# Silu from ScalarE's table, a two-row substitution and block copies in the token mixers of a hybrid decoder layer

## The chip, the core and the metric

The kernel runs on one core of a Trainium2 chip. The core has five engines that run their own instruction lists and wait for each other by semaphores: TensorE (PE in the profile; its weight loads are PEld), VectorE (DVE), ScalarE (ACT), GpSimd (POOL) and SyncE (SP), which here issues the DMAs. The metric is the device time of one execution in microseconds, as the median of several runs. All data are float32; the large matrix products are run as three products of split operands in the type fp32r.

## The reference

One decoder layer (DEPTH is 1) over 2048 tokens of width 1024. Cut to what the change touches:

```python
qkv = jax.nn.silu(causal_depthwise_conv(qkv, gdn_conv[i]))
q_a, k_a, v_a = jnp.split(qkv, 3, axis=-1)          # 4 heads of 128; q_a, k_a are L2-normed
g_dec = -jnp.exp(gdn_a_log[i]) * jax.nn.softplus(a_gdn + gdn_dt_bias[i])
o_a = gated_delta_rule_chunked(q_a, k_a, v_a, g_dec, beta)
o_a = o_a * lax.rsqrt(mean(o_a * o_a) + EPS) * gdn_norm[i] * jax.nn.silu(z_gdn)
...
f = lb + (1 - lb) * sigmoid(f_pre)                  # log_f of the reference
k_b = (1.0 - lb) * jax.nn.sigmoid(-f_pre)
o_b = hgrn2_chunked(jax.nn.silu(q_hg), k_b, i_hg, log_f)
o_b = o_b * lax.rsqrt(mean(o_b * o_b) + EPS) * hgrn_norm[i] * jax.nn.silu(g_hg)
```

The gated delta rule needs, for every chunk of tokens, the solution of a unit lower triangular system. The mixers are followed by an output projection, a squared-ReLU MLP and a gated embedding; the change leaves these alone.

## The kernel before

The work goes in four quarters `q` of 512 tokens (`QT`), each of four chunks (`NC`) of 128. Activations lie transposed: features on the partitions, tokens along the free axis.

The trace falls into stages. Up to about 45 us the embedding products and the first operands are made. From there to about 1180 us runs the input projection with the mixers inside it. Then come the output projection (to about 1440 us), and the two MLP products and the gate product (to the end). The change lies in the mixers and in the constants that they read.

**Projection and mixers.** The list `works` holds 33 products for each quarter: one for the decays, and for each of four heads eight (`KINDS`: k, q, v, z of the delta rule; f, i, q, g of HGRN2). One work is 24 matmuls on L927, in `SPT` = 3 parts, and after each part `tick()` advances a clock and runs one step of every generator that is due. The due times stand in the tuples `A_STEPS`, `I_STEPS` and `B_STEPS` (`A_LAST`, `B_LAST` for the last head): the generator `gdn_mixer` of a head is advanced at these distances from the head's start, `hgrn_mixer` likewise. A head's eight works take 24 steps and its delta-rule mixer ends at step 59, so the mixers of two or three heads are open at once.

The order of PE's instructions is that of the program (`manual_schedule`), and so is SP's inside the loop: what a step issues to PE stands there between the matmuls of the projection, and when it has to wait, everything behind it waits. The order on DVE, ACT and POOL is made by a planner ahead of time, from when it reckons that operands are ready; on the chip each engine takes its list in order.

**The activations.** There is no silu function in use: `silu2` (L475) computes Tanh of half the argument on ACT and then `(th + 1) * x` on DVE (L479), which is twice the silu. `conv_silu` (L490) uses it for k, q and v, `to_hq` (L789) for HGRN2's queries. `gate` (L509) does the same for z and g with a Copy on ACT that carries half the norm's gain (L514) and a product on DVE (L515). The factor of two is made up for by `4 * EPS` and the like in the norms.

**The delta-rule head (`gdn_mixer`).** The decays come by DMA into `gf`. The matrix `e` of decay ratios is made by four DVE instructions (L552, one a chunk) and one Exp (L553). `u`, the strictly triangular system, is formed on DVE (L591) from matmuls of k with itself. Its diagonal blocks of 32 (`SB`) go through DRAM into the tile `sys`, so that 16 blocks lie on 128 partitions; rows are then solved one after the other, each by a product (L615) and a sum (L616) on DVE, 31 pairs for a head. The result goes through DRAM into `xx`, which holds for each chunk the inverse (right half) and its transpose (left half, made by DVE's transposes on L630). Two levels, 32 and 64, join the blocks: `um` gets the off-diagonal blocks of `u` (ACT, L634), PE forms `psp` (L638), ACT copies it to `pt` (L640), PE multiplies again into `psd` (L647, L648, L655), and DVE adds `psd` to `xx` (L651, L656). The matmuls stream all 128 columns. Then the four chunks follow in sequence: `psa`, `r` on DVE (L664), `psb` with the inverse, `w` on ACT (L669), the state `S` on DVE (L674).

**The HGRN2 head (`hgrn_mixer`).** Levels 1 to 64 (`LEVELS`) build the attention of a chunk. On each level PE multiplies k with the odd blocks of q (L726), DVE scales the odd blocks of q (L727) and the even blocks of k (L729), and a predicated copy with the level's mask puts the result into `att` (L732). The masks are stored for all four chunks, 256 columns each. `to_f` (L767) makes f and k from a Tanh by two DVE instructions (L773, L774).

**The end of a head (`finish`, L518).** The squared output is summed by PE, its inverse root is spread through DRAM, and DVE multiplies the gated output by it (L530).

## Time and profile before

| | us |
|---|---|
| median of 3 runs | 2867.37 (2864.68 to 2872.71) |
| the profiled execution, device time | 2865.62 |
| its span | 2863.8 |
| PE busy / DVE busy / ACT busy in the span | 2773.0 / 2158.2 / 1331.2 |
| PE busy in L927, the input projection | 791.2 |
| DVE busy in L615 and L616, the substitution | 136.1 and 111.0 |

Rows of the profile read as follows. A group has the line, the engine, the operation, output and inputs by their names (with the head's part of the name cut, so `psp_g` stands for all heads), the shapes and the count; then the busy time in us, the mean of one in ns, and the idle time of the engine just before it with the engine or DMA that ended it. A row of the list of waits has who waited, for whom, the total in us, how often, and the longest. A row of the timeline has start and length in us and, in brackets, the idle time before it. A float32 matmul shows as two instructions. Matmuls overlap, so the distance from start to start tells more than the length. The granted clock is TensorE's, 1.00 at full speed.

### The profile page before, as it was taken

To read this page: it belongs to the slowest core of one execution; us is meant where nothing else is said; L and a number is where in the kernel's file an instruction comes from. 1 tells how busy PE (TensorE), PEld (TensorE's weight loads), DVE (VectorE), ACT (ScalarE), POOL (GpSimd) and SP (SyncE) were. 2 spreads that over 40 slices of the span, in tenths; PEclk is the share of its full clock that TensorE was granted. 3 is DMA by queue.
4 is the path that set the end of the run, shared out by engine and by line. 5 is a ranking of instruction groups with operands and counts; after the bars stand their busy time and mean duration, and the time that the engine had idled before them with its cause. 6 is when DMAs were issued, how large, how long until landed. Compare 5 with 4: busy or idle time off the path is not lost.

```text
span 2863.8 us, 39544 instructions
## 1 busy us (share of the span) xinstructions
PE 2773.0 (97%) x13361; PEld 2293.7 (80%) x13361; DVE 2158.2 (75%) x4712; ACT 1331.2 (46%) x2460; POOL 108.7 (4%) x104
## 2 busy tenths in 40 slices
PE   7899999999999999999989999999999999999999
PEld 5688788888888888777768887888888888887887
DVE  6688787887878887758887886776787765567675
ACT  6354334333333333457555655554555445465431
POOL 0000000000000000000000000000100000001000
PEclk9999999999999999999999999999999999999999
DMA  7666667655665666587755646666564446577573
GB/s 254 223 222 205 215 213 246 201 199 201 224 195 190 212 199 196 159 284 247 258 173 192 229 166 209 217 212 210 193 210 139 148 157 213 188 255 239 196 230 116
DMA packets 268602, 589.70 MB, mean 206 GB/s; under 512 B 55642, under 2 KB 59960, under 8 KB 249072
## 3 DMA queue, kind: packets, MB, share of 16 engines
q1 hardware_dynamic: 268400, 587.18, 61.5%
q8 instruction: 106, 1.74, 0.3%
q14 instruction: 96, 0.79, 0.1%
HBM read 420.14 MB, written 166.92 MB: 205 GB/s over the span
## 4 chain that ended last, share of the span: by engine, by line
PE 46%; DVE 3%; DMA 3%; issue 2%; ACT 2%; POOL 0%; SPq 0%; DVEq 0%; ACTq 0%; POOLq 0%
PE u L996 21%; PE d L996 18%; PE mmg L996 6%; DMA da<-sumd 1%; DMA raw_out<-in_w_out_dram 1%; DMA xo<-in_xT_dram 1%; DMA b<-h1d 0%; PE mmo L996 0%; DVE w_out L162 0%; DVE t L162 0%; ACT L1033 0%; ACT L1032 0%; ACT w_out L161 0%; DVE b L1143 0%; POOL acc_y L225 0%
## 5 line engine op out<-in xcount | busy, mean ns | idle before, releaser
L927 PE MATMUL mm<-xt,w 128*128 128x512 f32 x3072 | 791.2, 405 | 2.6 <-ACT w L161 1.2
L927 PEld LDWEIGHTS mm<-xt,w 128*128 128x128 f32 x3072 | 564.6, 191 | 122.8 <-ACT w L161 1.6
L996 PE MATMUL d<-db,da 128*128 128x512 f32 x2688 | 613.0, 390 | 4.2 <-DVE db L215 3.2
L996 PE MATMUL u<-t,wu 128*128 128x512 f32 x2604 | 603.4, 393 | 3.3 <-ACT wu L161 3.2
L996 PEld LDWEIGHTS d<-db,da 128*128 128x128 f32 x2688 | 504.0, 188 | 112.6 <-DVE db L215 5.8
L996 PEld LDWEIGHTS u<-t,wu 128*128 128x128 f32 x2604 | 488.8, 188 | 117.2 <-ACT wu L161 4.1
L215 DVE TENSOR_TENSOR db<-db 128x512 fp32r<-128x512 f32 x224 | 160.8, 718 | 69.9 <-ACT db L214 69.4
L1325 DVE TENSOR_TENSOR u<-u,u 128x512 f32<-128x512 f32 x224 | 150.8, 684 | 72.1 <-PE u L996 71.0
L996 PE MATMUL mmo<-mixT,w_out 128*128 128x512 f32 x720 | 171.5, 398 | 9.1 <-DVE w_out L162 6.8
L214 ACT ACTIVATE db<-db 128x512 fp32r<-128x512 f32 x224 | 140.9, 629 | 78.7 <-DMA db<-hid 76.3
L996 PE MATMUL mmg<-h2T,wg 128*128 128x512 f32 x768 | 177.5, 393 | 0.0
L996 PEld LDWEIGHTS mmo<-mixT,w_out 128*128 128x128 f32 x720 | 137.0, 191 | 42.6 <-DVE w_out L162 8.5
L996 PEld LDWEIGHTS mmg<-h2T,wg 128*128 128x128 f32 x768 | 144.2, 188 | 32.8
L1366 ACT ACTIVATE u<-u 128x512 f32<-128x512 f32 x128 | 80.9, 632 | 179.6 <-DVE u L1325 179.2
L162 DVE TENSOR_TENSOR da<-da 128x512 fp32r<-128x512 f32 x128 | 94.3, 737 | 91.0 <-ACT da L161 90.5
L615 DVE TENSOR_TENSOR pr_g<-xs_g,sys_g 128x4 f32<-128x4 f32 (+30 forms) x496 | 136.1, 274 | 29.3 <-DMA sys_g<-ud_g 19.3
L161 ACT ACTIVATE da<-da 128x512 fp32r<-128x512 f32 x128 | 80.5, 629 | 140.0 <-DMA da<-sumd 117.3
L616 DVE TENSOR_REDUCE xs_g<-pr_g 128x4 f32<-128x8 f32 (+30 forms) x496 | 111.0, 224 | 9.8
L161 ACT ACTIVATE wu<-a 128x512 fp32r<-128x512 f32 x124 | 73.9, 622 | 46.7 <-DMA a<-in_w_up_dram 44.6
L225 POOL TENSOR_TENSOR acc_y<-acc_y,sq_y 128x512 f32<-128x512 f32 x28 | 38.7, 1382 | 1389.4 <-ACT sq_y L224 1389.4
L162 DVE TENSOR_TENSOR wu<-a,wu 128x512 fp32r<-128x512 f32 x124 | 84.9, 688 | 4.0 <-ACT wu L161 4.0
L726 PE MATMUL at_h<-q_h,k_h 128*128 128x64 f32 x640 | 82.6, 273 | 3.2 <-DVE tail_g L548 1.7
(364 smaller groups left out, 3893.1 us busy)
## 6 DMA issues: line engine op xcount, KB each, us to landing
w<-cache_in SPq DMA_DIRECT2D x96, 1024.0 KB
db<-hid SPq DMA_DIRECT2D x224, 256.0 KB
cache_in<-w SPq DMA_DIRECT2D x32, 1024.0 KB
hid<-u SPq DMA_DIRECT2D x128, 256.0 KB
da<-sumd SPq DMA_DIRECT2D x128, 256.0 KB
a<-in_w_up_dram SPq DMA_DIRECT2D x124, 256.0 KB
hid<-ht SPq DMA_DIRECT2D x96, 256.0 KB
dr<-in_w_down_dram SPq DMA_DIRECT2D x96, 256.0 KB
```

The costliest lines, as they stand in the source:

```text
L161: S.activation(t[:, 0], raw, AF.Copy)
L162: eng.tensor_tensor(t[:, 1], raw, t[:, 0], ALU.subtract)
L214: S.activation(t[:, 0], plain(t), AF.Copy)
L215: V.tensor_tensor(t[:, 1], plain(t), t[:, 0], ALU.subtract)
L225: eng.tensor_tensor(acc, acc, sq, ALU.add)
L615: V.tensor_tensor(pr[:, :, 0:i], xs[:, :, 0:i], sys[:, None, 0:i, i].broadcast_to([P, GC, i]), ALU.mult)
L616: V.tensor_reduce(xs[:, :, i], pr[:, :, 0 : i + 1], AX.X, ALU.add)
L726: PE.matmul(ps[:, c, :], k[:, blk(c)], odd, start=True, stop=True)
L927: PE.matmul(ps, *terms[i], start=i == 0, stop=i == nt - 1)
L996: PE.matmul(ps, a, b, start=start, stop=stop)
L1325: V.tensor_tensor(c[new], c[old], ps, ALU.add)
L1366: S.activation(c[k], c[k], AF.Relu)
```

## The change

- `silu2` goes. k, q, v and HGRN2's q take the function Silu on ACT; `gate` becomes one Silu, and the norm's gain is multiplied in at `finish`. The factors of 2 and 4 go from the norms.
- `e` is made by one DVE addition over all chunks and four Exp with the negative decay as bias.
- The substitution solves two rows a step: one product and one sum for rows i and i+1, and a third small instruction that adds row i's share to row i+1.
- In the inverse, `psp` and `psd` are formed for the wanted half of the columns only, `part` is a strided view of the tile `half`, and ACT copies the new blocks into `xx` where DVE added whole tiles.
- HGRN2's q and k lie in one tile `qk`, and one DVE instruction scales both. f and k come from ACT (Identity).
- The masks are stored once and broadcast over the chunks.

```diff
-N_CONST = C_MASK + 2 * len(LEVELS)
+N_CONST = C_MASK + (len(LEVELS) + 1) // 2
...
+            V.tensor_scalar(gcol[:, :, 4:8], gcol[:, :, 0:4], -1.0, None, ALU.mult)
...
-            silu2(y, acc, name)
+            S.activation(y, acc, AF.Silu)
...
-            S.activation(th, ps, AF.Tanh, scale=0.5)
-            S.activation(zt, ps, AF.Copy, scale=gate_w[:, n : n + 1])
-            V.scalar_tensor_tensor(zt, th, 1.0, zt, ALU.add, ALU.mult)
+            S.activation(zt, ps, AF.Silu)
...
-            V.tensor_tensor(og, og, rsb, ALU.mult)
+            V.scalar_tensor_tensor(og, og, col(R_GNORM if h < 4 else R_HNORM), rsb, ALU.mult, ALU.mult)
...
+            V.tensor_tensor(e, gf, over_chunks(negm), ALU.add)
             for c in range(NC):
-                V.scalar_tensor_tensor(e[:, c, :], gf[:, c, :], gc[:, c : c + 1], negm, ALU.subtract, ALU.add)
-            S.activation(e, e, AF.Exp)
+                S.activation(e[:, c, :], e[:, c, :], AF.Exp, bias=gcol[:, c, 4 + h : 5 + h])
             S.activation(gf, gf, AF.Exp)
...
-            for i in range(1, SB):
-                V.tensor_tensor(pr[:, :, 0:i], xs[:, :, 0:i], sys[:, None, 0:i, i].broadcast_to([P, GC, i]), ALU.mult)
-                V.tensor_reduce(xs[:, :, i], pr[:, :, 0 : i + 1], AX.X, ALU.add)
-                if i % 4 == 3:
+            for i in range(0, SB, 2):
+                if i:
+                    V.tensor_tensor(pr[:, :, :, 0:i], xs[:, None, :, 0:i].broadcast_to([P, 2, GC, i]),
+                                    sys[:, 0:i, i : i + 2].rearrange("p j two -> p two j")[:, :, None, :]
+                                    .broadcast_to([P, 2, GC, i]), ALU.mult)
+                    V.tensor_reduce(xs[:, :, i : i + 2].rearrange("p g two -> p two g"), pr[:, :, :, 0 : i + 1],
+                                    AX.X, ALU.add)
+                V.scalar_tensor_tensor(xs[:, :, i + 1], xs[:, :, i], sys[:, i, i + 1 : i + 2], xs[:, :, i + 1],
+                                       ALU.mult, ALU.add)
+                if i % 4 == 2:
                     yield
...
+                psp = bank(f"psp_{n}_{lev}", pp)[:, : QT // 2].rearrange("p (c b s) -> p c b s", c=NC, s=s)
+                left = xx[:, :, :P].rearrange("p c (b two s) -> p c b two s", two=2, s=s)[:, :, :, 0]
+                right = xx[:, :, P:].rearrange("p c (b two s) -> p c b two s", two=2, s=s)[:, :, :, 1]
+                part = half.rearrange("p c (b two s) -> p c b two s", two=2, s=s)[:, :, :, 0]
                 for c in range(NC):
-                    PE.matmul(psp[:, blk(c)], um[lev][:, c, :], xx[:, c, :P], start=True, stop=True)
-                pt = m2.tile([P, NC, P], F32, tag="pt", name=f"pt_{n}_{lev}", bufs=1)
-                S.activation(flat(pt), psp, AF.Copy)
+                    PE.matmul(psp[:, c], um[lev][:, c, :], left[:, c], start=True, stop=True)
+                S.activation(part, psp, AF.Copy)
                 yield
...
+                psd = bank(f"psd_{n}_{lev}", pp).rearrange("p (c two b s) -> p c two b s", c=NC, two=2, s=s)
+                for c in range(NC):
+                    if lev == 5:
+                        PE.matmul(psd[:, c, 0], xx[:, c, P:], part[:, c], start=True, stop=True)
+                    PE.matmul(psd[:, c, 1], half[:, c, :], right[:, c], start=True, stop=True)
+                for i in range(P // (2 * s)):
+                    o = 2 * s * i
+                    if lev == 5:
+                        S.activation(left[o + s : o + 2 * s, :, i], psd[o + s : o + 2 * s, :, 0, i], AF.Copy)
+                    S.activation(right[o : o + s, :, i], psd[o : o + s, :, 1, i], AF.Copy)
...
-                V.tensor_tensor(qv[:, :, 1, :], qv[:, :, 1, :],
-                                gv[:, :, 0:1].broadcast_to([P, nb, s]), ALU.mult)
-                V.tensor_tensor(kv[:, :, 0, :], kv[:, :, 0, :],
-                                gv[:, :, 1:2].broadcast_to([P, nb, s]), ALU.mult)
+                sides = bass.AP(qk.tensor, qk.offset + s, [qk.ap[0], [QT - s, 2], [2 * s, nb], [1, s]])
+                V.tensor_tensor(sides, sides, gv.rearrange("p n two -> p two n")[:, :, :, None]
+                                .broadcast_to([P, 2, nb, s]), ALU.mult)
...
-            V.tensor_scalar(f, th, ha[:, h : h + 1], hb[:, h : h + 1], ALU.mult, ALU.add)
-            V.tensor_scalar(k, th, hna[:, h : h + 1], ha[:, h : h + 1], ALU.mult, ALU.add)
+            S.activation(f, th, AF.Identity, scale=ha[:, h : h + 1], bias=hb[:, h : h + 1])
+            S.activation(qk[:, 1], th, AF.Identity, scale=hna[:, h : h + 1], bias=ha[:, h : h + 1])
...
-            silu2(qq, ps, f"qh{q}_{h}")
-            b["q"] = qq
+            S.activation(b["qk"][:, 0], ps, AF.Silu)
```

## The prediction, made before the result was known

> **What bounds the kernel now.** I read three views in this order: the page's busy shares, the busy times of the mixer stage alone, and the list of what TensorE waited for there. First the page, then the stage from 45 to 1215 us (columns: stretch, length, then busy us and count for PE, PEld, DVE, ACT, POOL, then granted clock, DMA share, GB/s):

> ```profile
> PE 2773.0 (97%) x13361; PEld 2293.7 (80%) x13361; DVE 2158.2 (75%) x4712; ACT 1331.2 (46%) x2460; POOL 108.7 (4%) x104
> ```

> ```profile
> 45.00:1215.00 1170.00, 1125.79 (x6234) 956.71 (x6232) 937.58 (x2817) 446.89 (x1008) 64.17 (x67) 0.98 0.62 206
> ```

> The whole diff lies in this stage. PE is busy for 1125.8 of its 1170 us, so the change can win only the 44.2 us in which PE stands still, the time in which PE runs at a reduced clock, and matmul work itself. DVE is at 80%, ACT at 38%: taking load from DVE is worth nothing by itself; it is worth what PE now waits for DVE. That is the next view (45 to 1210 us; total, times, longest):

> ```profile
> PE psp_g L638 <- DVE xx_g L630: 17.6, 4, 10.6
> PE psb_g L667 <- DVE r_g L664: 12.9, 19, 1.3
> PE pso_h L748 <- DVE S_h L747: 3.2, 1, 3.2
> PE psp_g L638 <- DVE xx_g L651: 1.7, 1, 1.7
> PE at_h L726 <- DVE k_h L729: 1.3, 1, 1.3
> ```

> Nearly all of it is DVE arriving late. L630 is the end of the substitution (its result comes back through DRAM and is transposed), L651 the correction in the inverse. The five long stalls, in order of time (start, length, the wait in brackets), and the granted clock around them:

> ```profile
> 132.77 2.05 PE L638 MATMUL psp_g<-xx_g,um 128*128 128x128 f32 x8 [10.65 <-DVE xx_g L630]
> ...
> 318.29 0.77 PE L748 MATMUL pso_h<-q_h,S_h 128*128 128x128 f32 x2 [3.17 <-DVE S_h L747]
> ...
> 347.67 1.16 PE L638 MATMUL psp_g<-xx_g,um 128*128 128x128 f32 x8 [2.45 <-DVE xx_g L630]
> ...
> 629.07 2.07 PE L638 MATMUL psp_g<-xx_g,um 128*128 128x128 f32 x8 [2.11 <-DVE xx_g L630]
> ...
> 1202.50 0.71 PE L638 MATMUL psp_g<-xx_g,um 128*128 128x128 f32 x4 [1.66 <-DVE xx_g L651]
> ```

> ```profile
> 120.00:140.00 20.00, 9.35 (x42) 7.99 (x41) 10.96 (x32) 5.11 (x12) 0.00 (x0) 0.74 0.41 133
> 310.00:330.00 20.00, 16.68 (x85) 13.80 (x83) 18.65 (x56) 8.60 (x16) 0.00 (x0) 0.91 0.71 224
> 340.00:360.00 20.00, 17.55 (x86) 14.59 (x85) 13.55 (x37) 4.94 (x8) 1.01 (x1) 0.83 0.57 169
> 620.00:640.00 20.00, 17.89 (x73) 14.78 (x73) 12.51 (x35) 6.18 (x10) 1.01 (x1) 0.74 0.41 151
> 1200.00:1210.00 10.00, 7.01 (x39) 6.09 (x37) 6.31 (x13) 5.64 (x10) 0.00 (x0) 0.83 0.97 331
> ```

> A stall costs twice. Around each, the clock (third from the end) falls: lost are 0.26 x 20 = 5.2, 0.09 x 20 = 1.8, 0.17 x 20 = 3.4, 0.26 x 20 = 5.2 and 0.17 x 10 = 1.7 us, together 17.3 us. The wait of 2.11 us at 629 cost 5.2 us more in slow matmuls.

> [...]

> **The change, part by part.** PE first. All 20 matmuls of the inverse per GDN head (5 groups of four, each matmul two instructions) stream 64 columns instead of 128; 16 heads make 80 groups.

> ```profile
> 787.78 1.05 PE L638 MATMUL psp_g<-xx_g,um 128*128 128x128 f32 x8
> 788.67 1.00 PE L726 MATMUL at_h<-q_h,k_h 128*128 128x64 f32 x8
> 789.51 0.44 PE L588 MATMUL kk_g<-y_kg 128*128 128x128 f32 x2
> ```

> By start to start, eight of 128 columns take 0.89 us and eight of 64 take 0.84. Half the columns do not save half the time. (a): 80 x 0.05 = 4 us; bounds 0 and 80 x 0.45 = 36, if it scaled with columns. I take 4, because the 64-column row has the very form.

> DVE loses the silu products and gate products (first row L479, second L515, stage 45 to 1215, DVE busy and count), and then these groups (busy, mean ns, idle before):

> ```profile
> 45.00:1215.00 1170.00, 43.87 (x64) 0.98 0.62 206
> ...
> 45.00:1215.00 1170.00, 22.00 (x32) 0.98 0.62 206
> ```

> ```profile
> L615 DVE TENSOR_TENSOR pr_g<-xs_g,sys_g 128x4 f32<-128x4 f32 (+30 forms) x496 | 136.1, 274 | 29.3 <-DMA sys_g<-ud_g 19.3
> L616 DVE TENSOR_REDUCE xs_g<-pr_g 128x4 f32<-128x8 f32 (+30 forms) x496 | 111.0, 224 | 9.8
> ...
> L727 DVE TENSOR_TENSOR q_h<-q_h,gg_h 128x256 f32<-128x256 f32 x96 | 40.5, 422 | 15.4 <-PE at_h L726 14.5 <-ACT hb_h L699 0.3
> L729 DVE TENSOR_TENSOR k_h<-k_h,gg_h 128x256 f32<-128x256 f32 x96 | 40.3, 419 | 0.0
> L651 DVE TENSOR_TENSOR xx_g<-xx_g,psd_g 128x512 f32<-128x512 f32 x32 | 21.7, 683 | 8.7 <-PE psd_g L648 8.7
> L552 DVE SCALAR_TENSOR_TENSOR e_g<-gf_g,gcol,cst 128x128 f32<-128x128 f32 x64 | 19.2, 347 | 0.0
> L773 DVE TENSOR_SCALAR f_h<-th_h,ha,hb 128x512 f32<-128x512 f32 x16 | 8.8, 547 | 1.6
> ```

> - silu and gates: 43.9 + 22.0 = 65.9 us gone.
> - inverse: the adds move to ACT, 32 + 16 of 0.683 = 32.8 gone.
> - f and k move to ACT: 32 x 0.547 = 17.5 gone.
> - e: 64 x 0.347 by busy time 19.2, against 16 adds of 128x512 at 0.683 = 10.9: 8.3 gone.
> - one scaling for q and k: 40.5 + 40.3 against 96 x 0.683 = 65.6: 15.2 gone.
> - substitution: two of its products and one of its sums, at both ends of the sizes:

> ```profile
> 98.16 0.17 DVE L615 TENSOR_TENSOR pr_g<-xs_g,sys_g 128x4 f32<-128x4 f32 x1 [3.25 <-DMA sys_g<-ud_g]
> ...
> 126.53 0.37 DVE L615 TENSOR_TENSOR pr_g<-xs_g,sys_g 128x124 f32<-128x124 f32 x1
> ...
> 127.42 0.28 DVE L616 TENSOR_REDUCE xs_g<-pr_g 128x4 f32<-128x128 f32 x1
> ```

> A product is 0.163 us and 1.67 ns an element; a sum, from 0.28 at 128 and the mean 0.224 at 68, 0.16 and 0.93 ns. After the change a head has 15 products of 8i elements (i = 2, 4 .. 30; 1920 in all): 15 x 0.163 + 3.2 = 5.6; 15 sums of 2040 elements: 15 x 0.16 + 1.9 = 4.3; 16 single columns of 4 elements, between 0.17 (the smallest product) and 0.35 (the scalar form at 128 elements), I take 0.22: 3.5. That is 13.4 against (136.1 + 111.0) / 16 = 15.4 us, so 32 us less over 16 heads; at 0.35 nothing is won. The data moved are the same; only the count falls, from 62 to 46.

> The products with the norm gain in `finish` (32) become the scalar form, some 2 us more. Sum for DVE: 65.9 + 32.8 + 17.5 + 8.3 + 15.2 + 32 - 2 = 170 us less, 80% down to 66%.

> ACT (stage rows; the last is a table load, seen where Tanh follows the decays' Ln):

> ```profile
> L514 ACT ACTIVATE zt_gh<-mm,gate_w 128x512 f32<-128x512 f32 x16 | 10.9, 682 | 0.0
> L553 ACT ACTIVATE e_g<-e_g 128x512 f32<-128x512 f32 x16 | 10.2, 638 | 1.5 <-DVE e_g L552 1.5
> L568 ACT ACTIVATE kt_g<-t_kg,tail_g 128x128 f32<-128x128 f32 x64 | 24.3, 379 | 0.2
> L634 ACT ACTIVATE um<-u_g 32x128 f32<-32x128 f32 x32 | 9.8, 307 | 43.8 <-DVE u_g L591 43.4
> L478 ACT ACT_TABLE_LOAD x4 | 5.1, 1283 | 1.6 <-DVE acc_kg L497 1.1 <-DVE xx_g L630 0.3
> ```

> 32 gate copies go (-21.8), 32 affine copies for f and k come (+21.8 at the same price); Exp of e by chunk 64 x 0.379 - 10.2 = +14; block copies 80, at 0.307 = +24.6; half-size `part` -5. Then the tables: nothing in this trace has Silu, so a head costs between no load (Silu beside Exp) and four (Exp of `cd`, Silu of q, Exp of `tail` and `e`, Silu of v, if ACT takes them as they become ready). I take four, the cautious end: 64 x 1.283 = 82 us. ACT: +116 us, 38% to 48%. It does not become the bound; what counts is where it is late.

> What PE gets: (b) the first head's stall of 10.65: between 98.16 and 127.42 DVE runs the substitution with other work in its gaps. It loses 2.0 us of its own, some 0.5 in fewer gaps, and four silu or gate products of 0.687 = 2.7: 5.2 us. The clock is still lost. (c) the stalls at 318, 347 and 629 are at most 3.2 us late, against 170 / 16 = 10.6 us of DVE work taken away per head: gone, with their clock, 7.7 + 10.4 = 18.1. (d) at 1202, 1.66 + 1.3 and 1.7 of clock: 3 of 4.7, as ACT's copies may be late there instead. (e) r, 12.9 us in 19 waits, is a queue behind other DVE work; half, 6. Gains: 4 + 5.2 + 18.1 + 3 + 6 = 36.3. If each wait stayed, 4; if all 44.2 us and the 17.3 went, with 4: 65.5.

> (f) What ACT newly delays. One head's inverse today: the last correction matmul, the next product, and ACT's busy run ending between:

> ```profile
> 567.64 0.39 PE L648 MATMUL psd_g<-xx_g,pt_g 128*128 128x128 f32 x2
> ...
> 572.49 1.05 PE L638 MATMUL psp_g<-xx_g,um 128*128 128x128 f32 x8
> ```

> ```profile
> 568.30 0.68 ACT L581 ACTIVATE q_g<-y_qg 128x512 f32<-128x512 f32 x1
> ```

> Behind ACT's run stand now the block copies, and PE's product waits for them; behind that product the projection's matmuls wait, since PE runs in order. The run ends at 568.98; two loads (2.57) and e (0.9) more make it 572.4; four copies make 573.7: 1.2 us late. Ahead of the run, the copies would be done at 569.3, with 3 us to spare. I take the middle, 0.6 x 16 = 10 us; ends 0 and 19.

> Sum: 2865.62 (the profiled run, 1.75 below the median of 2867.37) - 36.3 + 10 = 2839; against the median 2841.

> **Rivals.**
> 1. ACT takes DVE's place (slower). The place is the product at 572.49. If lateness passes about 2 us, the row at 620 prices it at 2.1 + 5.2 = 7.3 us a head. It decides from 36.3 / 7.3 = 5 heads of 16; at 8 heads: 2867 + 58 - 36 = 2889. For it: ACT's run and the copies meet once per head. Against: ACT idles most of the stage, and loads that stand ahead of a wait are hidden in it. Chance 0.16.
> 2. Relief is hidden (same). The waits on DVE are partly DMA landings behind it, as the first head's 3.25 us before its first product; then only (a) and part of (e) arrive, 8 us, and (f) takes them: 2866. Chance 0.13.
> 3. Silu needs no other table than Exp (faster). (f) shrinks to about nothing: 2831. Chance 0.12.
> 4. [...] Chance 0.04.
> [...]

> **How the numbers follow.** The forecast has 0.55, the rivals 0.16, 0.13, 0.12, 0.04. Faster by over 0.3% (8.6 us, about what this kernel's runs can tell): 0.55 + 0.12 = 0.67. Same 0.13; slower 0.20. Predicted 2841. The range goes from 2812 (rival 3 with most of the remaining waits gone) to 2889 (rival 1 at eight heads).

> **What would show it.** In the changed trace: DVE about 770 us and ACT about 560 in the stage, table loads near 64 there; psp's wait for L630 near 5 us in one place; clock 1.0 around the later heads; r's wait near 6. Wrong would be: PE waiting for the block copies or for w on ACT in many heads with the clock falling after each; more than four loads a head; or the old waits standing with a shorter DVE list.

## The result, and the profile after

The changed kernel takes 2846.87 us (median of 4 runs, 2845.4 to 2849.48), the kernel before 2867.07 us in the same comparison: a ratio of 0.9928, 95% interval 0.9911 to 0.9945. It is 20 us faster. The profiled execution of the changed kernel took 2849.48 us (span 2847.7), that of the kernel before 2865.62.

First the page of the changed kernel, then its mixer stage from 45 to 1195 us, and for the same window that of the kernel before (columns as in the prediction: busy us and count for PE, PEld, DVE, ACT, POOL, then granted clock, DMA share, GB/s).

```profile
PE 2770.9 (97%) x13361; PEld 2297.4 (81%) x13361; DVE 2036.2 (72%) x4140; ACT 1431.1 (50%) x2639; POOL 110.5 (4%) x104
```

```profile
45.00:1195.00 1150.00, 1118.19 (x6268) 960.92 (x6268) 816.99 (x2252) 549.06 (x1191) 65.96 (x67) 0.99 0.64 211
```

```profile
45.00:1195.00 1150.00, 1109.00 (x6136) 942.01 (x6134) 923.25 (x2789) 436.65 (x990) 62.20 (x66) 0.99 0.62 206
```

In equal time PE does 132 matmul instructions more. What PE waits for has changed its kind, in the list of waits of the changed kernel from 45 to 1210 us:

```profile
PE psb_g L663 <- DVE r_g L660: 9.7, 16, 1.4
PE psp_g L640 <- ACT xx_g L651: 7.8, 5, 3.3
PE mm L922 <- ACT zt_zg L505: 4.6, 1, 4.6
PE mme L186 <- ACT sq_e L222: 3.6, 2, 2.0
PE psp_g L640 <- DVE xx_g L628: 2.2, 3, 1.5
```

The wait of the inverse's first product for the substitution (L638 for L630 before, L640 for L628 now) has fallen from 17.6 to 2.2 us. The new long ones are waits for ACT: the block copies of the inverse (L651), and the gate (L505), ahead of which ACT stands 2.12 us at a DMA for a weight tile and then loads a table (1.28 us). The longest of these, in order of time (start, length, the wait in brackets):

```profile
84.50 3.63 PE L922 MATMUL mm<-xt,w 128*128 128x512 f32 x8 [4.63 <-ACT zt_zg L505]
...
275.20 1.42 PE L640 MATMUL psp_g<-xx_g,um 128*128 128x64 f32 x8 [1.81 <-ACT xx_g L651]
...
426.11 1.97 PE L640 MATMUL psp_g<-xx_g,um 128*128 128x64 f32 x8 [3.33 <-ACT xx_g L651]
```

Where the time went by stage can be read from the first matmul of the output projection, which ends the mixers (groups of the kernel before and of the changed one: minimum, median and largest duration in ns, first and last start in us):

```profile
L956 PE MATMUL mmo<-mixT,w_out x48: 390/394/479, 1230.2 to 1244.9; 128*128 128x512 f32 x48
```

```profile
L951 PE MATMUL mmo<-mixT,w_out x48: 388/392/481, 1202.1 to 1216.7; 128*128 128x512 f32 x48
```

The mixers end 28.1 us earlier, the span only 16.1 us. So 12 us are given back in stages that the diff does not touch; the part on the prediction splits both numbers.

### The profile page after: what moved, and what is told of

The parts are those of the page before. It is cut to its first block, busy times and chain, and to the rows that moved or that the text cites. A ratio compares the mean times of both kernels' runs of the same rounds, so it can differ in the third digit from the quotient of the medians.

```text
span 2847.7 us, 39125 instructions
## 1 busy us (share of the span) xinstructions
PE 2770.9 (97%) x13361; PEld 2297.4 (81%) x13361; DVE 2036.2 (72%) x4140; ACT 1431.1 (50%) x2639; POOL 110.5 (4%) x104
## 4 chain that ended last, share of the span: by engine, by line
PE 48%; DMA 4%; DVE 3%; issue 2%; ACT 2%; POOL 0%; SPq 0%; DVEq 0%; POOLq 0%; ACTq 0%
PE u L991 21%; PE d L991 19%; PE mmg L991 6%; PE mmo L991 1%; DMA da<-sumd 1%; DMA xo<-in_xT_dram 1%; DMA b<-h1d 1%; DMA mixT<-mixd 0%; DMA raw_out<-in_w_out_dram 0%; DVE t L160 0%; ACT L1028 0%; DVE b L1138 0%; DVE w_out L160 0%; ACT L1027 0%; DMA rsb_n<-row 0%
## 5 line engine op out<-in xcount | busy, mean ns | idle before, releaser
L922 PE MATMUL mm<-xt,w 128*128 128x512 f32 x3072 | 777.5, 401 | 4.6 <-ACT zt_zg L505 4.6
L922 PEld LDWEIGHTS mm<-xt,w 128*128 128x128 f32 x3072 | 561.2, 189 | 115.0 <-ACT zt_zg L505 5.1
L159 ACT ACTIVATE da<-da 128x512 fp32r<-128x512 f32 x128 | 80.5, 629 | 136.0 <-DMA da<-sumd 115.2
L725 DVE TENSOR_TENSOR qk_h<-qk_h,gg_h 128x512 f32<-128x512 f32 x96 | 66.1, 689 | 74.3 <-PE at_h L722 74.2
L159 ACT ACTIVATE wu<-a 128x512 fp32r<-128x512 f32 x124 | 74.1, 624 | 47.2 <-DMA a<-in_w_up_dram 45.9
L608 DVE TENSOR_TENSOR pr_g<-xs_g,sys_g 128x16 f32<-128x16 f32 (+14 forms) x240 | 94.0, 392 | 5.3
L722 PE MATMUL at_h<-qk_h 128*128 128x64 f32 x640 | 85.6, 278 | 0.4 <-DVE qk_h L725 0.4
```

The lines of the kernel that those rows point to most:

```text
L159: S.activation(t[:, 0], raw, AF.Copy)
L608: V.tensor_tensor(pr[:, :, :, 0:i], xs[:, None, :, 0:i].broadcast_to([P, 2, GC, i]), sys[:, 0:i, i : i + 2].rearrange("p j two -> p two j" ...
L722: PE.matmul(ps[:, c, :], k[:, blk(c)], odd, start=True, stop=True)
L725: V.tensor_tensor(sides, sides, gv.rearrange("p n two -> p two n")[:, :, :, None] .broadcast_to([P, 2, nb, s]), ALU.mult)
L922: PE.matmul(ps, *terms[i], start=i == 0, stop=i == nt - 1)
```

## The experiments

All ratios are to the kernel before on the same chip. The last column is the start of the first output-projection matmul in the run's trace, as above; it tells of the mixers alone, with the start of the program in it.

| run | median us | ratio to before (95%) | output projection from, us |
|---|---|---|---|
| the changed kernel again | 2844.69 | 0.9902 (0.9887 to 0.9918) | 1203.0 |
| old silu | 2846.9 | 0.9911 (0.9896 to 0.9926) | 1208.1 |
| old substitution | 2869.07 | 0.9993 (0.9983 to 1.0003) | 1225.4 |
| old inverse | 2837.04 | 0.9877 (0.9863 to 0.9892) | 1193.3 |
| substitution alone, in the kernel before | 2853.08 | 0.9935 (0.9922 to 0.9948) | 1214.0 |
| block copies on DVE | 2842.26 | 0.9892 (0.9876 to 0.9908) | 1197.6 |
| no table switch | 2831.38 | 0.9862 (0.9847 to 0.9878) | 1188.0 |
| old silu and old inverse | 2842.76 | 0.9899 (0.9884 to 0.9913) | 1201.8 |
| old small parts | 2834.18 | 0.9891 (0.9875 to 0.9907) | 1189.2 |
| old inverse, one Exp | 2828.89 | 0.9873 (0.9858 to 0.9888) | 1189.6 |
| the same, Squares later | 2829.19 | 0.9872 (0.9856 to 0.9888) | 1189.2 |
| the kernel before, inverse a step later | 2853.05 | 0.9953 (0.9941 to 0.9965) | 1214.4 |

The kernel before took 2871.99 us beside the first four, 2870.97 beside the next four and 2863.52 beside the last four, so medians and the last column are compared within a group, and ratios across groups.

### The changed kernel again

No edit.

> The changed kernel as it is, in more rounds and beside the others, so that its ratio to the kernel before is known more closely: 0.9928 (0.9911 to 0.9945) so far, 2847 us.

Measured 0.9902; the difference to the first comparison's 0.9928 is 0.0026, and the intervals overlap. This row is the measure for the next ones.

### Old silu

```diff
-            S.activation(y, acc, AF.Silu)
+            silu2(y, acc, name)
...
-            S.activation(zt, ps, AF.Silu)
+            S.activation(th, ps, AF.Tanh, scale=0.5)
+            S.activation(zt, ps, AF.Copy, scale=gate_w[:, n : n + 1])
+            V.scalar_tensor_tensor(zt, th, 1.0, zt, ALU.add, ALU.mult)
```

> The changed kernel with silu and the gates as before (Tanh on ACT, product on DVE), all else changed. DVE gets 66 us of products back, ACT loses some 52 table loads (67 us). Theory 1 (the gain is DVE arriving earlier): the first head's substitution ends 2.7 us later, r waits more, some stalls with their clock return: about +8 us, 2855. Rival (ACT's table loads and late copies give back what silu wins): 2847 or less, with PE's waits on ACT copies near 0.

0.9911 against 0.9902: no difference that these runs can tell, although DVE is busy for 868.77 us in the stage here, against 816.99. Silu takes about 50 us off DVE and brings nothing in the end. Against the trace of the row before, PE waits again for DVE (6.14 us at the first head, 6.13 us for `r` at 318 us), the waits for the block copies fall from 8.7 to 2.2 us, and the projection's matmuls keep another pace: one behind the other at full clock they start 233.4 ns apart, where the changed kernel has 230.0. More on the loads is told by the run without a table switch, and on the pace by the part on the prediction.

### Old substitution

```diff
-            for i in range(0, SB, 2):
...
+            for i in range(1, SB):
+                V.tensor_tensor(pr[:, :, 0:i], xs[:, :, 0:i], sys[:, None, 0:i, i].broadcast_to([P, GC, i]), ALU.mult)
+                V.tensor_reduce(xs[:, :, i], pr[:, :, 0 : i + 1], AX.X, ALU.add)
```

> The changed kernel with the substitution row by row as before. DVE gets 62 instead of 46 small instructions a head, by the traces 247.1 instead of 222.2 us in all. Theory 1: the substitution ends 2 to 3 us later in each head; the first head's stall comes back in part, some 3 us and 3.4 us of half clock: about +7, 2854. Rival (with the silu products gone DVE has room enough, rows do not matter): 2847 within 3.

This one part decides: without it the whole change is worth nothing (0.9993), far more than the 7 us of theory 1, and the rival is out. Its stage, and its list of waits:

```profile
45.00:1195.00 1150.00, 1109.56 (x6179) 952.35 (x6177) 824.87 (x2483) 534.49 (x1164) 63.33 (x66) 0.98 0.63 206
```

```profile
PE psp_g L632 <- DVE xx_g L620: 13.7, 4, 4.5
PE psb_g L655 <- DVE r_g L652: 7.8, 14, 1.4
PE mm L914 <- ACT hist L492: 6.3, 1, 6.3
PE psp_g L632 <- ACT xx_g L643: 5.1, 5, 2.1
```

DVE is at 824.87 us, 98 less than in the kernel before and nearly as low as in the changed one. Yet the wait for the substitution is back, 13.7 us in 4 places. The first head's is 4.32 us, where the kernel before has 10.65, so there the load counts. The other three are those of the last heads of the first three quarters, 4.54, 1.36 and 3.45 us, where the kernel before has 2.45, 2.11 and 2.37 (the last at 916.20 us). In these heads the stretch from the substitution's first product to its last sum takes 37.3, 31.6 and 33.8 us, against 35.4, 34.4 and 33.9. So in these heads it is not the load of DVE as a whole that makes the product late.

### Old inverse

```diff
-                psp = bank(f"psp_{n}_{lev}", pp)[:, : QT // 2].rearrange("p (c b s) -> p c b s", c=NC, s=s)
+                psp = bank(f"psp_{n}_{lev}", pp)
...
-                    S.activation(right[o : o + s, :, i], psd[o : o + s, :, 1, i], AF.Copy)
+                    V.tensor_tensor(xx[:, :, P:], xx[:, :, P:], psd.rearrange("p (c n) -> p c n", n=P), ALU.add)
```

> The changed kernel with the inverse as before: 128 columns, DVE adds in place of ACT's block copies. PE gets 3 us more matmul work, DVE 33 us more, ACT 80 copies less. Theory 1 with rival 1 of the prediction (the block copies on ACT are late in five places, 7.8 us and the clock after three of them, some 5 us): -13 + 3 + 2, about 2839. Other theory (the inverse's DVE adds were among what was late): +5 or more, 2852.

0.9877, by 0.0025 or some 7 us better than the changed kernel; the intervals overlap a little (0.9887 to 0.9892). Its mixers end 9.7 us earlier (1193.3 against 1203.0). From 45 us to there PE stands still 5.0 us less and loses 6.7 us less to half clock, and its matmuls take 2.0 us more: theory 1 in kind and size. This kernel has no block copies, and its list of waits from 45 to 1195 us has no row for DVE's adds, which take their place:

```profile
PE mm L923 <- ACT hist L491: 8.6, 5, 5.7
...
PE psp_g L635 <- DVE xx_g L627: 1.7, 2, 1.3
```

### Substitution alone

The kernel before, with only the two-row loop of the diff shown above.

> The kernel before with nothing changed but the substitution in two-row steps. Chain theory (the length of the substitution's chain of dependent DVE instructions in the heads at the quarter ends decides, about 3 us a head shorter with 46 instructions than with 62): most of the gain, ratio 0.990 to 0.994. Load theory (DVE's total load decides; 25 of the 121 us taken from DVE in the stage): a fifth of the gain, 0.998.

0.9935, as the chain theory had it: about 19 us of the 28 that the changed kernel gains by its ratio (0.0065 and 0.0098 of 2871). DVE stays as loaded as before, 919.30 of 1150 us:

```profile
45.00:1195.00 1150.00, 1116.18 (x6215) 948.46 (x6214) 919.30 (x2557) 444.95 (x1003) 66.95 (x66) 0.99 0.63 209
340.00:360.00 20.00, 20.00 (x127) 17.63 (x126) 15.40 (x39) 9.27 (x26) 2.34 (x2) 1.00 0.57 185
620.00:640.00 20.00, 20.00 (x127) 17.78 (x126) 14.07 (x35) 6.77 (x23) 2.06 (x2) 1.00 0.53 196
```

The places of the stalls at 347 and 629 us have a clock of 1.00 now (0.83 and 0.74 before). The reason can be read in the stretch from a head's first product to its last sum. Each pair of rows is of DVE: first the instructions that write or read `xs` alone, then all of them. The kernel before, head 4 (the last of the first quarter):

```profile
307.20:342.60 35.40, 15.30 (x62) 0.95 0.70 231
```

```profile
307.20:342.60 35.40, 33.61 (x107) 0.95 0.70 231
```

The run with the new substitution alone, the same head:

```profile
300.30:329.20 28.90, 13.98 (x46) 0.94 0.77 247
```

```profile
300.30:329.20 28.90, 27.80 (x80) 0.94 0.77 247
```

The chain's own work falls by only 1.3 us, but the chain gets 6.5 us shorter: 34 foreign instructions stand between its links instead of 45. Over 16 heads the mean length goes from 27.0 to 22.7 us, at 22.7 foreign instructions instead of 28.6. DVE's list is fixed ahead of time and each link needs the one before, so the planner puts other work behind a link; a chain with 16 links less has fewer such places. That the foreign work falls with the links is shown; that the planner reckons a gap behind each link is the author's estimate, and no run shows it.

### Block copies on DVE

```diff
-                    S.activation(right[o : o + s, :, i], psd[o : o + s, :, 1, i], AF.Copy)
+                    V.tensor_copy(right[o : o + s, :, i], psd[o : o + s, :, 1, i])
```

> The changed kernel with the block copies of the inverse on DVE instead of ACT, all else changed, the halved columns too. If the copies' place in ACT's queue is what the inverse loses by (8.7 us of waits in five places and the half clock after three): ratio 0.986 to 0.988, as with the old inverse or a little better, and the wait of psp on ACT gone. If it is the halved form itself: 0.990, unchanged.

0.9892, inside the intervals of both the changed kernel and the old inverse: not settled. The wait for the block copies is gone from its list of waits, and no row for the copies on DVE has come. The longest row is one for ACT's `hist` (45 to 1195 us), of which the second trace of the changed kernel has 4.5 us too:

```profile
PE mm L922 <- ACT hist L492: 7.3, 3, 4.3
```

### No table switch

```diff
-            S.activation(zt, ps, AF.Silu)
+            S.activation(zt, ps, AF.Tanh)
```

The same in `conv_silu` and for HGRN2's q.

> The changed kernel with the function Tanh wherever it has Silu, so the activations of the mixers are not the reference's; Tanh runs from the table that Exp leaves loaded, so the 52 table loads between Exp and Silu go and nothing else changes. If the loads are hidden in ACT's idle time: 0.989 to 0.990, 0 to 3 us faster than the changed kernel. If they are what makes ACT late at the block copies: 8 us or more, 0.987 or lower.

0.9862 against 0.9902: the switches cost 0.0040 of 2871, or 11.5 us. The table loads, in the groups of ACT from 45 to 1195 us, in the changed kernel, where seven lines have 59 (the two largest groups; 7 of the 59 belong to the decays):

```profile
L494 ACT ACT_TABLE_LOAD x26 | 33.4, 1283 | 15.9 <-DVE acc_qg L491 5.9 <-DVE acc_vg L491 5.9 <-DVE acc_kg L491 3.5
L537 ACT ACT_TABLE_LOAD x16 | 20.5, 1283 | 0.3
```

and with Tanh in the place of Silu (8):

```profile
L457 ACT ACT_TABLE_LOAD x4 | 5.1, 1283 | 0.1
L494 ACT ACT_TABLE_LOAD x4 | 5.1, 1283 | 3.5 <-DVE acc_kg L491 3.5
```

In the changed kernel's mixers a load stands at each of the 24 places where a Silu follows an Exp and at each of the 24 where an Exp follows a Silu; in those of the kernel before, none stands at the 52 where a Tanh follows an Exp or an Exp a Tanh. 51 loads less, 65.4 us of ACT, are worth 11.5 us here: most of their time is hidden. By the ratios, Silu without the loads would win 0.0049 against the old silu (0.9911), and the loads take 0.0040 of it back: this is why Silu is neutral, the relief of DVE and the loads on ACT come out about even.

### Old silu and old inverse

Both edits together.

> The changed kernel with silu, gates and inverse as before; the substitution, e, f and k on ACT and the single scaling stay. If silu is neutral and the old inverse wins 7 us: 0.988. If the old inverse wins only while DVE is free of the silu products (it puts 33 us of adds back on DVE, silu 66): 0.992 or higher.

0.9899, not to be told from the changed kernel, and between the two forecasts: the old inverse's 7 us do not show without Silu. What is left is the substitution and the small parts (`e` by chunk on ACT, f and k on ACT, one scaling for q and k), and compared with the substitution alone (0.9935) the small parts seemed to be worth 0.0036 or 10 us. The next run put that to the test.

### Old small parts

```diff
-                S.activation(e[:, c, :], e[:, c, :], AF.Exp, bias=gcol[:, c, 4 + h : 5 + h])
+                V.scalar_tensor_tensor(e[:, c, :], gf[:, c, :], gc[:, c : c + 1], negm, ALU.subtract, ALU.add)
+            S.activation(e, e, AF.Exp)
...
-            S.activation(f, th, AF.Identity, scale=ha[:, h : h + 1], bias=hb[:, h : h + 1])
+            V.tensor_scalar(f, th, ha[:, h : h + 1], hb[:, h : h + 1], ALU.mult, ALU.add)
```

> The changed kernel with four small parts as before: e by scalar_tensor_tensor on VectorE and one Exp, no negated gcol, f and the key gate on VectorE, two scalings for q and k. Theory (the remainder of the gain, that the two-row substitution alone does not bring, is worth about 10 us and lies in these parts): ratio near 0.994, 2854 us where the kernel before takes 2870, and the first output-projection matmul 8 to 10 us later than the 1203 us of the changed kernel. Rival (these parts are hidden, and the remainder is a joint effect): ratio 0.990, within 3 us of the changed kernel.

0.9891: the rival holds. Without the small parts the kernel is not slower. So the 10 us were not theirs. The runs that take back one other part, or two, differ from the changed kernel by 0.0025 at most, and all their ratios lie below that of the substitution alone: what the substitution leaves can be won by one part or by another, and they do not add up. The substitution alone has DVE at 919.30 us in the stage and a wait of 7.52 us in the first head left; it is by far the longest that its timeline shows for PE in the mixers:

```profile
128.53 2.05 PE L646 MATMUL psp_g<-xx_g,um 128*128 128x128 f32 x8 [7.52 <-DVE xx_g L638]
```

With the old small parts, and so with silu and the inverse changed, DVE is at 850.66 us and the first head's wait at 2.27.

### Old inverse, one Exp

The old inverse, and:

```diff
-            S.activation(cd, glast, AF.Exp)
-            V.tensor_tensor(tail, glast, gc, ALU.subtract)
-            S.activation(tail, tail, AF.Exp)
...
+                V.scalar_tensor_tensor(e[:, c, :], gf[:, c, :], gc[:, c : c + 1], negm, ALU.subtract, ALU.add)
+            S.activation(eg, eg, AF.Exp)
+            S.activation(cd, glast, AF.Copy)
...
+                S.activation(ktail[:, c, :], psk[:, blk(c)], AF.Copy, scale=e[:, c, P - 1 : P])
```

`e` and `gf` lie in one tile `eg`; `cd` and `tail` are columns of the result.

> The changed kernel with the old inverse, and with one Exp over a joined tile of e and gf; the decay over a chunk is a column of that result, copied, and tail is the last column of e, so that the Exps of cd and tail, which each called for a table load behind a Silu, go. Theory (the inverse part costs some 7 us, and each table load in a wait of TensorE costs too: 3.25 loads a head go towards 2): ratio 0.984 to 0.985, about 2826 us, with fewer than 40 table loads in the mixers. Rival (the loads are hidden once the block copies are gone): 0.988 as with the old inverse alone.

The table loads between Silu and Exp fall from 52 to 36, as the two groups show:

```profile
L492 ACT ACT_TABLE_LOAD x20 | 25.7, 1283 | 2.7 <-DVE acc_kg L489 1.1 <-DVE acc_vg L489 0.5 <-DVE ncc_g L559 0.5
L537 ACT ACT_TABLE_LOAD x16 | 20.5, 1283 | 0.6 <-DMA eg_g<-gd 0.3
```

The ratio is 0.9873, that of the old inverse (0.9877): the rival holds, and the loads taken away were hidden ones, unless the additions for `e` that go back to DVE in this edit cost as much as they win; no run parts the two. Apart from the run with Tanh for Silu, it is the fastest by its ratio, together with the next: 34.6 us below the kernel before on its chip. Against the changed kernel it is 0.0029 lower, with intervals that overlap by 0.0001 only.

### The same, Squares later

```diff
-                    S.activation(t, t, AF.Square, accum_out=ss2[:, a, c : c + 1])
+                    if late:
+                        u, w = late.pop()
+                        S.activation(u, u, AF.Square, accum_out=w)
+                    late.append((t, ss2[:, a, c : c + 1]))
```

> The kernel of the run before, with the Squares of the row norms of x one step behind their DMAs, so that ScalarE does not stand at a DMA with other work behind it. Theory (ScalarE's order, in which work that TensorE waits for stands behind a DMA wait as at 426 us, costs 1 to 4 us): ratio 0.983 to 0.984. Rival (these stalls were only where the block copies stood behind it): the same ratio as the run before, within 0.1%.

0.9872, the same: the rival again. It was meant for the stall at 426 us, where in the changed kernel ACT's list reads

```profile
421.88 0.63 ACT L425 ACTIVATE xs<-xs 128x512 f32<-128x512 f32 x1 [3.75 <-DMA xs<-in_x_dram]
...
425.79 0.27 ACT L651 ACTIVATE xx_g<-psd_g 32x128 f32<-32x128 f32 x1
```

ACT stands 3.75 us at a DMA, then works without a gap up to the block copies, and PE's product comes at 426.11. With the old inverse no block copy stands there, and in the run before PE has no wait at its product (417.46 us). Later Squares with the new inverse were not tried.

### The kernel before, inverse a step later

```diff
-A_STEPS = ((3, 6, 7, 9, 10, 12, 14, 16, 17, 18, 19, 20, 21, 22, 24, 26, 28, 30, 32, 34, 36)
-            + tuple(range(38, 50)) + (50, 52, 54, 55, 57, 59))
+A_STEPS = ((3, 6, 7, 9, 10, 12, 14, 16, 17, 18, 19, 20, 21, 22, 24, 26, 29, 31, 33, 35, 37)
+            + tuple(range(39, 51)) + (51, 53, 55, 56, 58, 60))
```

> The kernel before, with the inverse and the chunk steps of each GDN head issued one step later in the plan, nothing else: VectorE and ScalarE have the work of before. Theory (the substitution is a chain with a deadline, the first product of the inverse; a later deadline helps as a shorter chain does): the waits of that product at 347 and 629 us go with their clock, the first one is about 3 us shorter, ratio 0.994 to 0.995, about 2855 us. Rival (VectorE's load makes TensorE late, wherever the deadline lies): 1.000 or above, the waits turning up at the steps behind.

0.9953 (0.9941 to 0.9965): the first theory's 0.994 to 0.995 is in the interval, the rival's 1.000 is not. DVE and ACT have the 4712 and 2460 instructions of the kernel before, and the stretch from the substitution's first product to its last sum is as long: 26.7 us on average (27.0 before), 35.7, 33.1 and 34.2 us in the last heads of the first three quarters. From 45 us to the output projection PE stands still 9.2 us less than in the kernel before and loses 8.3 us less to half clock; with the substitution alone these are 9.8 and 8.4. The windows at the old stalls, and the first head's wait:

```profile
340.00:360.00 20.00, 19.88 (x119) 17.36 (x120) 16.24 (x42) 7.22 (x15) 1.02 (x2) 1.00 0.61 202
620.00:640.00 20.00, 20.00 (x116) 17.10 (x116) 16.92 (x43) 6.31 (x14) 1.01 (x1) 1.00 0.57 198
```

```profile
134.00 2.05 PE L638 MATMUL psp_g<-xx_g,um 128*128 128x128 f32 x8 [9.61 <-DVE xx_g L630]
```

Both later stalls and their clock are gone. The first wait shrank by 1.0 us, not 3. So the substitution is a chain with a deadline, the step at which its first product stands in PE's list: the same waits go by a shorter chain or by a later deadline. By the ratios the first brings 19 us and the second 13; the intervals overlap.

## Why the prediction was right or wrong

2841 us was predicted, 2846.87 measured, on the predicted side of no change and 5.9 us above. The mechanism was half right: the place (PE at the inverse's first product, priced with its clock) and the new waits on ACT were right, the reason why the place clears was not. That the time comes so near is in part luck: 26 us were forecast for the mixers and 28.1 came, but 10 of these lie in matmul time, for which the sum had 4, and the 12 given back later had no term. Rivals 1 and 2 did not come: PE is late at block copies in 5 places and not in 8 heads; the gain is more than 8 us. The chance of 0.04 has nothing in the runs behind it: no row has a load of more than 1283 ns. Rival 3 is excluded by the loads: 28 stand ahead of a Silu and 24 ahead of an Exp in the heads. What rival 2 forecast, no gain, is what all parts but the substitution bring (0.9993), though not for its reason, DMA landings.

- **(a)**, 4 us from halved columns. Eight 64-column matmuls of the first product stand 0.84 us apart from start to start (551.21 to 552.05 us), and the sixteen of level 32's correction take 1.73 us (557.12 to 558.85): against 0.89 for eight and 1.78 for sixteen in the kernel before, that is 0.05 for a group of four alone and 0.05 for the pair of groups on level 32. With four such steps a head it is 3.4 us, not 4. The saving by columns (36) did not come:

```profile
551.21 1.00 PE L640 MATMUL psp_g<-xx_g,um 128*128 128x64 f32 x8
552.05 1.06 PE L722 MATMUL at_h<-qk_h 128*128 128x64 f32 x8
...
557.12 0.33 PE L646 MATMUL psd_g<-half,xx_g 128*128 128x64 f32 x2
...
558.85 1.06 PE L722 MATMUL at_h<-qk_h 128*128 128x64 f32 x8
```

- **(b)**, the first head: 5.2 of 10.65 us predicted, with the clock still lost. All but 0.5 us of the wait went, and its clock. The clock was priced too high, though: in the kernel before, half clock ran from 127.2 to 137.5 us, and the product stands at 132.77, so of the 5.2 us some 2.3 were work at half speed; the rest lay inside the wait. The term was mis-sized: it put the fewer gaps at 0.5 us. The stretch fell from 29.5 to 20.9 us; the foreign instructions in it from 25 (87 less 62) to 9 (55 less 46). It takes both parts: the new loop alone leaves 7.52 us of the wait, all other parts without it 4.32. Of DVE, the kernel before and the changed one:

```profile
98.16:127.70 29.54, 27.91 (x87) 0.93 0.56 205
```

```profile
96.80:117.70 20.90, 18.53 (x55) 1.00 0.77 271
```

- **(c)**, 18.1 us from the later stalls: the stalls at 318, 347 and 629 went, as predicted, but not because of "170 / 16 = 10.6 us of DVE work taken away per head". This is the step that failed in its reason: with that relief and the old loop they stayed (3.17, 4.54 and 1.36 us), and without the relief, with the new loop or with a later deadline, they went. The prediction's list of long stalls also left out the wait for L630 at 916 us, which is longer than the one at 629 and cost no clock:

```profile
916.20 1.16 PE L638 MATMUL psp_g<-xx_g,um 128*128 128x128 f32 x8 [2.37 <-DVE xx_g L630]
```

- **(d)**, 3 us at 1202: the wait there is gone, but at this end of the mixers PE now waits 3.6 us for `sq_e` on ACT, so little or nothing was won.
- **(e)**, r: 6 of 12.9 us predicted, 3.2 measured (9.7 left, in the same window).
- **(f)**, 10 us lost to ACT. Waits for the block copies are 7.8 us and for the gate 4.6. Around the copies' stalls the clock is lower as well:

```profile
200.00:220.00 20.00, 18.70 (x103) 16.29 (x102) 12.02 (x28) 13.46 (x37) 2.02 (x2) 0.91 0.57 200
270.00:290.00 20.00, 18.19 (x92) 16.13 (x91) 12.70 (x33) 13.41 (x37) 2.01 (x2) 0.83 0.57 201
420.00:440.00 20.00, 16.67 (x87) 14.94 (x85) 9.80 (x26) 10.89 (x33) 1.01 (x1) 0.83 0.79 281
```

These are 1.8 + 3.4 + 3.4 = 8.6 us. With the 12.4 of the waits, (f) is about 21, twice what it was put at; the half clock behind the gate's wait (0.91 from 80 to 100 us) adds 1.8. By experiments, the table loads alone cost 11.5 us and the inverse's part some 7. The mechanism, copies behind ACT's run, was as predicted; that a DMA wait ahead of the run (3.75 us) makes it later was not in the sum.
- **The loads of the engines.** DVE's groups of the two traces add up to 2400.5 and 2235.3 us, 165 less against the 170 predicted, but its busy time fell by 2158.2 - 2036.2 = 122 us: neighbouring instructions overlap, and durations that are added up count the overlap twice. ACT rose by 99.9 us (116 predicted), with 52 loads between Silu and Exp where 64 were predicted: ACT took some of them in one visit. The substitution takes (94.0 + 70.6 + 57.7) / 16 = 13.9 us a head (13.4 predicted):

```profile
L608 DVE TENSOR_TENSOR pr_g<-xs_g,sys_g 128x16 f32<-128x16 f32 (+14 forms) x240 | 94.0, 392 | 5.3
L611 DVE TENSOR_REDUCE xs_g<-pr_g 128x8 f32<-128x24 f32 (+14 forms) x240 | 70.6, 294 | 5.0
L613 DVE SCALAR_TENSOR_TENSOR xs_g<-xs_g,sys_g 128x4 f32<-128x4 f32 x256 | 57.7, 225 | 8.7 <-DMA sys_g<-ud_g 3.3
```

- **What the sum had no term for**: 12 us given back behind the mixers. From the first output-projection matmul to the end, the kernel before takes 1633.6 us and the changed one 1645.6 (1644.9 in its second trace). PE's time can be split in three, from the busy times and the granted clock of the two traces: standing still, lost to half clock, and the rest, the matmuls' own time. Where the granted clock is 0.50, the pairs of L578 and L579 start 0.43 us apart in the changed kernel (279 to 281 us), at 1.00 they start 0.22 us apart (139 to 141 us); so half of PE's busy time there is counted as lost.

| us | still | lost to half clock | rest |
|---|---|---|---|
| up to the output projection, before | 62.3 | 17.9 | 1150.0 |
| the same, changed | 46.8 | 15.3 | 1140.0 |
| from there to the end, before | 28.5 | 4.8 | 1600.3 |
| the same, changed | 30.0 | 9.6 | 1606.0 |

So 10.0 of the 28.1 us won and 5.7 of the 12 lost are matmul time, at 13361 instructions in both. Besides the inverse (a), it is the pace of matmuls that the diff does not touch. One behind the other at full clock, the projection's (L927 before, L922 now) start 233.4 ns apart before and 229.9 after, the first MLP product's 231.1 and 232.9. In 200 us of the latter, without a wait and at a clock of 1.00, PE does 869 before (first row) and 859 after (second):

```profile
1500.00:1700.00 200.00, 200.00 (x869) 162.91 (x868) 168.61 (x273) 113.90 (x189) 0.00 (x0) 1.00 0.59 201
```

```profile
1500.00:1700.00 200.00, 200.00 (x859) 161.40 (x858) 162.18 (x263) 112.68 (x186) 0.00 (x0) 1.00 0.54 188
```

The projection's pace goes with the form of silu and nothing else that was tried: the five kernels with the old form have 233.3 to 233.4 ns, the eight others, and the second trace of the changed one, 229.8 to 230.0. Taking Silu back alone costs 6.5 us of matmul time ahead of the output projection and wins 6.4 behind it. What in the form does it is not shown; no mixer runs beside the MLP, so it is not DVE's load in the mixers alone. Of the 12 us, 7.2 lie in the first MLP product, which lasts from 1427.5 to 1749.5 us before and from 1401.6 to 1730.8 after. Beside its start, the clock of before (first row) and after (second):

```profile
1436.00:1476.00 40.00, 34.96 (x140) 26.84 (x141) 29.55 (x48) 21.47 (x36) 0.00 (x0) 0.96 0.34 112
```

```profile
1410.00:1450.00 40.00, 33.61 (x122) 25.72 (x123) 28.28 (x46) 19.69 (x32) 0.00 (x0) 0.87 0.34 110
```

That is 1.6 against 5.2 us of lost clock. PE stands longer there after the change, 5.77 us against 4.33 for weights that ACT prepares (L159 now, L161 before), and its next stand, 2.53 against 2.44 us, costs clock after the change and none before. Why ACT is later there stays open. Other runs range from 1632.6 us (the kernel before with the later inverse) to 1645.7 (block copies on DVE).

## What to carry to other kernels

Where one engine's results are wanted at a fixed place in another's list, look at the length of the dependent chain in the loaded queue, foreign instructions included, before its busy share: here 16 links fewer, with 1.3 us of work in them, took 6.5 us off one head, and some 98 us of relief elsewhere did not do the same there. Try moving the deadline too: a changed tuple of due times, with no other edit, won 0.5%. Work that went to the idle engine was not free here: look for what stands ahead of it there, such as the table loads on ACT (11.5 us of the time) and the DMA wait of 3.75 us ahead of the block copies at 426 us. And look at the pace of instructions that the change does not touch before its gain is put down to waits (233.4 against 229.9 ns in the projection).

## What the runs showed of the hardware

```profile
912.28:915.69 3.41, 1.55 (x7) 0.93 (x5) 3.31 (x10) 0.48 (x2) 1.01 (x1) 1.00 0.38 77
625.56:628.97 3.41, 1.40 (x6) 0.77 (x5) 3.26 (x10) 0.43 (x2) 1.01 (x1) 1.00 0.40 79
628.97:639.21 10.24, 10.14 (x34) 8.70 (x35) 3.72 (x11) 2.51 (x3) 0.00 (x0) 0.50 0.56 228
```

So what these two waits cost in clock, 0 and 5.1 us, went with where they fell on the grid.

- A table load is 1283 ns in every group of the two traces, and the idle time put down to it is 0.0 to 0.3 us where no operand is late (L537, 16 loads: 0.3 in all). In the changed kernel's mixers ACT stands 18 ns ahead of a load and 11 ns behind it (medians of 59).
